# One decoder layer on one core: order of the first loads, merge weights by broadcast loads, 1/rms at the MLP's outputs, weight sums by DMA, and DVE's order at the end

## The chip, the cores and the metric

The kernel runs on one core of a Trainium2 chip. The metric is device time in microseconds (us) of one execution; lower is better. A core has five engines that run side by side, each through its own instructions in order: TensorE (PE: matrix products and transposes), VectorE (DVE), ScalarE (ACT), GpSimd (POOL) and SyncE (SP, which here only issues DMA transfers). They wait for one another through semaphores.

## The reference

One layer of a decoder over 512 tokens of width 1024, all in float32:

```python
h = rmsnorm(x, g_mix)
z = h @ w_in            # 9728 columns: retention q/k/v/gate, attention q/k/v of 3 groups, 2 merge gates
ret_branch = (silu(rg) * rmsnorm(retention(rotate(rq), rotate(rk), rv), ret_gn)) @ w_ret_out
aq, ak = rotate(rmsnorm(aq, q_gain)), rotate(rmsnorm(ak, k_gain))    # per head and group
outs, lses = [dilated_window_attention(aq[g], ak[g], av[g]) for g in 3 groups]
att_branch = sum_g(softmax(lses)[g] * outs[g]) @ w_att_out
x = x + (sig(gl_r + b) * ret_branch + sig(gl_a + b) * att_branch) @ w_o
x = x + square(relu(rmsnorm(x, g_mlp) @ w_up)) @ w_down             # 4096 wide
x = x + sig(rmsnorm(x, g_ple) @ w_ple_gate) * (p @ w_ple_proj)
```

`rmsnorm` divides each token's row by its root mean square and multiplies by a gain for each column.

## The kernel before

**Products.** Each float32 operand is split into two rounded parts, hi (a copy that rounds, on ACT, L228 for weights) and lo (the rest, on DVE, L229), and a product takes three matmuls: hi*hi, lo*hi, hi*lo (L261 to L263). One matmul has a 128 x 128 stationary part and 512 moving columns. Weights come in units of 512 KB (`raw`, 128 x 1024), listed beforehand in a plan; a unit holds 12 such matmuls in the MLP. Six raw buffers and four split buffers (`whi`, `wlo`) run ahead of TensorE: `fetch` issues loads on SP, `ahead` splits two units further than the product at hand has taken.

**Order.** The program is written as it would run on one thread, with a queue of postponed steps (`later(lag, ...)`) that are taken up one at each `tick` between matmuls; `force` brings a step forward. A scheduler then decides each engine's order, except for instructions that `pin` keeps in the order of the program. Each engine runs its list strictly in that order.

**Stages.** `setup` loads the gains as columns (`gcol`), the transposed x (`xr`) beside the first four weight units, and x by tokens (`x`). `load_tables` loads the rotation table (`rotc`), the mask, and, as six broadcast loads, the q and k gains into the tile `mg`, each also with its halves swapped. `first_panel` computes the first 512 columns of z without the norm's factor: 1/rms is a number per token, so it is applied as z leaves PSUM (`zn`, L552). That factor r comes from squares of x on ACT (L484), v on DVE (L487) and a power on POOL (L488). Then for each head the q and k rows are normed (v, r on POOL at L327, `zn` on DVE at L558), rotated (`ro`) with tables C and S (table times gain, L537), transposed by heads (`ph`) and copied (`hT`).

After the first attention group, `embed` loads p transposed (`praw`), splits it (`pT`, L467 and L468) and computes p @ w_ple_proj, which is kept in DRAM (`pp_dram`). Two more groups follow, then retention, during which `merge` weighs the three groups: for each head and group four transposes of a column of weights spread over 128 columns (`pc`, L699) put the weight of each token along the free axis, and DVE multiplies (`mt`, L702). `spread_factors` does the like for r (`r_free`, L497). `mix` computes gates, branch products and their sum; `tail` multiplies by w_o and adds to x.

**MLP.** The norm of x is applied before its transposes: squares on ACT, v and r, y = x * r (L366), four transposes (`pt`, L337), and hi and lo with the gain (L345, L346). The down product is done in four stages of seven products instead of eight (a Strassen-like scheme, `seven_gemm`): its weights are sums and differences of blocks. For a sum, a second raw unit is loaded and DVE adds it (L208); differences are made on DVE too (L205). The products' results are added to x on DVE (L905). As rows of x are complete in the last stage, `ready` starts the last norm and its transposes into h3, and `fin` computes the sigmoid, the product with pp, the sum and the store.

Of the kernel before, what the change touches and what calls it, by code (L numbers as in the profile page):

```python
# [75 lines left out]
class Block:  # L76
# [102 lines left out]
    def fetch(self, n):  # L179
        while len(self.raws) < min(len(self.plan), n):  # L180
# [12 lines left out]
            if add is not None:  # L193
                g0 = self.wraw.tile([P, 1024], F32, tag="raw", name=self.nm("raw2")).rearrange("p (k n) -> p k n", k=k)
                self.nc.sync.dma_start(g0, rows(add[0]))
            self.raws.append((raw, g0))

    def ahead(self, n):
        while len(self.loaded) < min(len(self.plan), self.used + n):
# [4 lines left out]
            if isinstance(src, tuple) and src[0] is None:  # L204
                self.nc.vector.tensor_tensor(raw, raw, self.raws[g0][0], op=ALU.subtract)  # L205
                g0 = None
            elif isinstance(src, tuple):
                self.nc.vector.tensor_tensor(raw, raw, g0, op=ALU.add)  # L208
                g0 = None
# [55 lines left out]
    def rows_gemm(self, act, nk, consume, perm=False, group=2, need=None, halves=False):  # L265
# [3 lines left out]
        for u0 in range(0, nu, group):  # L269
            us = self.units(min(group, nu - u0))  # L270
            for t in range(NT):
                if need is not None:
                    need(t)
# [56 lines left out]
    def split_T(self, src, t, gcol, c, dst):  # L330

        nc = self.nc
        for part in src:
            n = part.shape[1] // P
            ps = self.bank("pt")
# [33 lines left out]

    def new_act(self, nbig, s):  # L370
        return ([self.big(s + "h") for _ in range(nbig)], [self.big(s + "l") for _ in range(nbig)])


    def setup(self):
        nc, a = self.nc, self.a
        self.gcol = self.const.tile([P, 48], F32, name="gcol")
        nc.sync.dma_start(self.gcol, a["vec_cols"])
# [26 lines left out]
    def load_tables(self):  # L404
# [20 lines left out]
    def first_panel(self, consume):  # L425
# [23 lines left out]
        for k in range(KD // 2):  # L449
            for t in range(NT):  # L450
                part(t, k)
        self.token_factors()
        for t in range(NT):
# [3 lines left out]
            self.ahead(1 + t // 2)  # L457
# [3 lines left out]
    def embed(self):  # L461
        nc = self.nc
        pT = self.big("pT")
# [4 lines left out]
        nc.vector.tensor_tensor(R(lo), raw, hi, op=ALU.subtract)  # L468
        self.pp_dram = self.dram.tile([S, D], F32, name="pp_dram", tag="pp_dram")
# [8 lines left out]
    def token_factors(self):  # L478
# [3 lines left out]
        for t in range(NT):  # L482
            j = self.big("j").rearrange("p a b -> p (a b)")[:, :D] if t == 0 else j
            nc.scalar.activation(j, self.x_tiles[t], AF.Square, accum_out=ss[:, t : t + 1])  # L484
# [4 lines left out]
        d = self.dram.tile([S, 1], F32, name="r_dram", tag="r_dram")  # L489
# [4 lines left out]
    def spread_factors(self):  # L494
        ps = self.bank("pc")
# [3 lines left out]
        self.nc.scalar.activation(self.r_free, ps, AF.Copy)  # L499
# [162 lines left out]
    def merge(self, groups, oh, ol):  # L662
# [29 lines left out]
        accs = [None] * H  # L692
        nat = lambda ap: ap.rearrange("p (l r) -> p r l", r=DIL)

        def weigh(h, g):
            self.force(("att", g, NT - 1))
            ps = self.bank("pc")
            for r in range(DIL):
                nc.tensor.transpose(ps[:, r * P : (r + 1) * P],  # L699
                                    cs[g][:, r, h : h + 1].to_broadcast([P, P]), self.ident)  # L700
            t = self.tmp("mt")
            nc.vector.tensor_tensor(t, groups[g][0][:, h], ps, op=ALU.mult)  # L702
# [11 lines left out]
        for h in range(H):  # L714
            for g in range(NG):
                self.later(8, lambda h=h, g=g: weigh(h, g), ("O", h, g))
# [103 lines left out]
    def mix(self, A, O):  # L820
# [61 lines left out]
    def seven_gemm(self, U, xs, ready):  # L882
# [21 lines left out]
        def acc(x, v, op=ALU.add):  # L904
            nc.vector.tensor_tensor(x, x, v, op=op)  # L905
# [5 lines left out]
        for p in range(2):  # L911
# [3 lines left out]
            acc(X(0, 1, p), banks[3, p])  # L915
            acc(X(0, 1, p), banks[5, p], ALU.subtract)
        for u in range(2):
            product(2, 4, u, False, u == 1)
        for p in range(2):
            acc(X(1, 0, p), banks[4, p])  # L920
            acc(X(1, 1, p), banks[4, p], ALU.subtract)
        for u in range(2):
            product(1, 1, u, u == 0, u == 1)
        for p in range(2):
            acc(m4[p], banks[1, p])
            acc(X(0, 0, p), m4[p])
            acc(X(1, 1, p), m4[p])
        for u in range(2):
            product(7, 5, u, False, u == 1)
        for p in range(2):  # L930
            acc(X(0, 0, p), banks[5, p])
            if ready is not None:
                ready(p)
        for u in range(2):
            product(6, 3, u, False, u == 1)
        for p in range(2):
            acc(X(1, 1, p), banks[3, p])
            if ready is not None:
                ready(2 + p)


    def tail(self, mx):
# [59 lines left out]
        for half in range(2):  # L1002
# [70 lines left out]
```

## Time and profile before

| | |
|---|---|
| three runs | 1030.88, 1027.52, 1030.28 us; median 1030.28 |
| profiled execution | 1032.18 us, of which the span (first to last instruction) is 1030.4 |
| TensorE busy | 1010.3 us, 98% of the span |
| DVE, ACT, POOL busy | 654.1, 461.4, 50.3 us |
| mean granted TensorE clock | 0.992 |
| DMA | 130.91 MB, mean 127 GB/s |

How to read the rows. A row of a timeline has the start and duration in us, engine, line, operation, output<-inputs, and in brackets how long the engine had been idle and what ended the wait. A row of groups has line, engine, operation, names, shapes, count, then busy us and mean ns of one, then idle us before them. A window's row has from:to, its length, then for each engine asked for its busy us and count, then the granted clock, the share of time in which the 16 DMA engines were busy, and GB/s. A DMA issue row ends with KB and the median us from issue to landing. In the rows of the chain that ended last, the columns are start, us, and what the time was spent on. Matmuls overlap: a 128x512 matmul lasts 0.39 us in the rows, while the next starts earlier. At half clock it lasts 0.63.

### The profile page before, as it was taken

What the parts mean: (1) busy time and instruction counts of PE and PEld (TensorE: products, weight loads), DVE (VectorE), ACT (ScalarE), POOL (GpSimd) and SP (SyncE); (2) the same over time, 40 slices, a digit from 0 to 9 for tenths busy, and PEclk for the clock granted to TensorE, in tenths of its full rate; (3) what the DMA queues carried; (4) which work ended last, traced back from release to release, by engine and by line L of the source; (5) the groups of instructions that cost most, each with busy time, mean ns of one, the idle gap of its engine ahead of it and who ended that gap; (6) DMA issues with size and microseconds to landing.
All of it is one profiled execution on the core that took longest, in us unless ns stands there. A gap on an engine that the chain in (4) does not pass through costs nothing.

```text
span 1030.4 us, 12593 instructions
## 1 busy us (share of the span) xinstructions
PE 1010.3 (98%) x4778; PEld 847.3 (82%) x4778; DVE 654.1 (63%) x968; ACT 461.4 (45%) x898; POOL 50.3 (5%) x64
## 2 busy tenths in 40 slices
PE   9698999999999999999999999999999999999998
PEld 6587889988988788888888888988888888888877
DVE  4486557666578734555443444679769867867983
ACT  4553545454343332534332323664456355356461
POOL 0110011011000001000110010000000000000000
PEclk9898999999999999999999999999999999999999
DMA  9734322223221241222232431355744753845711
GB/s 319 179 100 138 104 82 82 82 63 122 83 82 41 83 118 46 82 82 82 82 107 98 166 108 54 116 171 174 238 160 136 234 178 117 262 157 189 244 63 56
DMA packets 85869, 130.91 MB, mean 127 GB/s; under 512 B 7472, under 2 KB 39728, under 8 KB 85808
## 3 DMA queue, kind: packets, MB, share of 16 engines
q1 hardware_dynamic: 85808, 130.10, 39.5%
q8 instruction: 37, 0.61, 0.3%
q14 instruction: 24, 0.20, 0.1%
HBM read 125.87 MB, written 4.21 MB: 126 GB/s over the span
## 4 chain that ended last, share of the span: by engine, by line
PE 83%; DVE 9%; DMA 3%; issue 2%; ACT 1%; POOL 1%; SPq 0%; ACTq 0%; DVEq 0%; POOLq 0%
PE pg L261 24%; PE pg L263 24%; PE pg L262 24%; DVE wlo L229 2%; DMA raw<-in_w_in 2%; PE pb L261 2%; PE pb L263 2%; PE pb L262 2%; PE po L640 1%; POOL r L327 1%; PE pt L337 1%; DMA rotc<-in_c_rot 1%; PE ph L523 1%; DVE ro L511 1%; PE sc L617 1%
## 5 line engine op out<-in xcount | busy, mean ns | idle before, releaser
L228 ACT ACTIVATE whi<-raw 128x1024 fp32r<-128x1024 f32 (+1 forms) x198 | 204.3, 1040 | 237.5 <-PE pg L263 100.2
L229 DVE TENSOR_TENSOR wlo<-raw,whi 128x1024 fp32r<-128x1024 f32 (+1 forms) x198 | 239.9, 1221 | 82.0 <-ACT whi L228 80.8
L261 PE MATMUL pg<-whi,hh 128*128 128x512 f32 x480 | 201.1, 420 | 9.1 <-ACT zn L552 8.5
L262 PE MATMUL pg<-wlo,hh 128*128 128x512 f32 x480 | 189.8, 395 | 0.0
L263 PE MATMUL pg<-whi,hl 128*128 128x512 f32 x480 | 189.6, 395 | 0.0
L261 PEld LDWEIGHTS pg<-whi,hh 128*128 128x128 f32 x480 | 99.3, 207 | 24.3 <-ACT zn L552 9.0
L263 PEld LDWEIGHTS pg<-whi,hl 128*128 128x128 f32 x480 | 99.0, 206 | 17.7
L262 PEld LDWEIGHTS pg<-wlo,hh 128*128 128x128 f32 x480 | 99.5, 207 | 14.1 <-DVE wlo L229 0.4
L261 PE MATMUL pg<-h2h,whi 128*128 128x512 f32 (+1 forms) x288 | 105.4, 367 | 0.0
L262 PE MATMUL pg<-h2l,whi 128*128 128x512 f32 (+1 forms) x288 | 105.2, 365 | 0.0
L263 PE MATMUL pg<-h2h,wlo 128*128 128x512 f32 (+1 forms) x288 | 105.2, 365 | 0.0
L327 POOL TENSOR_TENSOR r<-v,mhalf 128x4 f32<-128x4 f32 (+1 forms) x48 | 38.2, 796 | 780.1 <-DVE v L326 780.1
L263 PEld LDWEIGHTS pg<-h2h,wlo 128*128 128x128 f32 x288 | 54.3, 189 | 8.8
L262 PEld LDWEIGHTS pg<-h2l,whi 128*128 128x128 f32 x288 | 54.3, 189 | 8.7
L261 PEld LDWEIGHTS pg<-h2h,whi 128*128 128x128 f32 x288 | 54.2, 189 | 8.6
L261 PE MATMUL pg<-hh,whi 128*128 128x512 f32 x128 | 52.5, 410 | 0.0
L263 PE MATMUL pg<-hh,wlo 128*128 128x512 f32 x128 | 50.0, 390 | 0.0
L262 PE MATMUL pg<-hl,whi 128*128 128x512 f32 x128 | 49.9, 390 | 0.0
L261 PE MATMUL pg<-whi,uh 128*128 128x512 f32 x128 | 49.9, 390 | 0.0
L263 PE MATMUL pg<-whi,ul 128*128 128x512 f32 x128 | 49.9, 390 | 0.0
L262 PE MATMUL pg<-wlo,uh 128*128 128x512 f32 x128 | 49.8, 389 | 0.0
L208 DVE TENSOR_TENSOR raw<-raw,raw 128x1024 f32<-128x1024 f32 x32 | 39.0, 1220 | 11.3 <-DMA raw<-in_w_down 11.2
(179 smaller groups left out, 1669.9 us busy)
## 6 DMA issues: line engine op xcount, KB each, us to landing
raw<-in_w_down SPq DMA_DIRECT2D x80, 512.0 KB, 3.4
raw<-in_w_in SPq DMA_DIRECT2D x72, 512.0 KB, 3.8
raw<-in_w_up SPq DMA_DIRECT2D x32, 512.0 KB, 4.9
x<-in_x SPq DMA_DIRECT2D x8, 512.0 KB, 6.7
raw<-in_w_ret_out SPq DMA_DIRECT2D x8, 512.0 KB, 3.4
raw<-in_w_o SPq DMA_DIRECT2D x8, 512.0 KB, 3.3
raw<-in_w_ple_gate SPq DMA_DIRECT2D x8, 512.0 KB, 4.5
xr<-in_x_cols SPq DMA_DIRECT2D x8, 256.0 KB, 5.4
```

Of the source, the lines that this page charges most:

```text
L208: self.nc.vector.tensor_tensor(raw, raw, g0, op=ALU.add)
L228: self.pin(nc.scalar.activation(R(hi[:, i]), raw[:, i], AF.Copy))
L229: nc.vector.tensor_tensor(R(lo[:, i]), raw[:, i], hi[:, i], op=ALU.subtract)
L261: t.matmul(ps, sh, mh, start=first, stop=False, skip_group_check=more)
L262: t.matmul(ps, sh, ml, start=False, stop=False, skip_group_check=more)
L263: t.matmul(ps, sl, mh, start=False, stop=last, skip_group_check=more)
L327: self.nc.gpsimd.tensor_tensor(r, v, self.mhalf[:, :w], op=ALU.pow)
L337: nc.tensor.transpose(ps[:, k * P : (k + 1) * P], part[:, k * P : (k + 1) * P], self.ident)
L511: nc.vector.tensor_tensor(v4(t2)[:, :, o0 : o0 + 64], v4(zn)[:, :, i0 : i0 + 64], bc(Sn[:, o0 : o0 + 64], 64), op=ALU.mult)
L523: self.nc.tensor.transpose(ps[:, t * P : (t + 1) * P], rots[t][:, h * HD : (h + 1) * HD], self.ident)
L617: nc.tensor.matmul(sc[:, h * P : (h + 1) * P], qT[:, h, rs], kT[:, h, rs], start=True, stop=True)
L640: nc.tensor.matmul(po[:, h * P : (h + 1) * P], v[:, vt, h * HD : (h + 1) * HD], pt, start=b == 0, stop=b == len(blocks) - 1)
```

## The change

Five parts, which share a file but little code.

1. *First loads.* `gcol` is loaded from ACT's queue, and a tiny activation there loads ACT's table early. Weight units 4 and 5 are fetched before the tables (`fetch(6)`). The q and k gains come as one array that the host has arranged, in one broadcast load of 128 x 1536. The four squares are pinned ahead of the splits of units 4 and 5, which are done in halves. The load and split of p are moved from `embed` to `embed_operands`, after the first group's k projection.
2. *Merge weights.* The 48 weights of each token are transposed once, stored to DRAM, and come back as 12 broadcast loads (`cb`), each issued three weighings ahead. `r_free` is a broadcast load of r too.
3. *1/rms at the MLP's outputs.* The MLP's input is x times the gain row (`gr`), not yet divided. Since relu and square pass a positive factor on as its square, the accumulation multiplies each product by f = 1/v or -1/v per token (L948 after); the last norm's factor goes into the sigmoid's scale.
4. *Weight sums by DMA.* The second unit of a sum is added to the first by an accumulating DMA that GpSimd issues into the same buffer; the DVE add and the second buffer are gone.
5. *Order at the end.* From the last stage of `seven_gemm` on, ACT's and DVE's instructions keep the order of the program; halves of x are scaled and transposed as they are complete, some into other banks.

```diff
@@ fetch, ahead
             if add is not None:
-                g0 = self.wraw.tile([P, 1024], F32, tag="raw", name=self.nm("raw2")).rearrange("p (k n) -> p k n", k=k)
-                self.nc.sync.dma_start(g0, rows(add[0]))
+                self.nc.gpsimd.dma_start(raw, rows(add[0]), accum_op=ALU.add)
...
-            elif isinstance(src, tuple):
-                self.nc.vector.tensor_tensor(raw, raw, g0, op=ALU.add)
-                g0 = None
@@ new helpers
+    def gain_T(self, x, t, h, gain, dst, key, lag, bank=None):
+        y = self.tmp("y")
+        self.nc.vector.tensor_tensor(y, x[:, h * 512 : (h + 1) * 512], gain[h], op=ALU.mult)
+        self.later(lag, lambda: self.split_T([y], t, None, 4 * h, dst, bank), (key, t, h))
+    def mean_squares(self, x, v):
+        ss = self.small(2, "ss")
+        for h in range(2):
+            j = self.tmp("j")
+            nc.scalar.activation(j, x[:, h * 512 : (h + 1) * 512], AF.Square, accum_out=ss[:, h : h + 1])
+        s1 = self.small(1, "s1")
+        nc.vector.tensor_tensor(s1, ss[:, 0:1], ss[:, 1:2], op=ALU.add)
+        nc.vector.tensor_scalar(v, s1, 1.0 / D, EPS, op0=ALU.mult, op1=ALU.add)
@@ setup, load_tables
-        nc.sync.dma_start(self.gcol, a["vec_cols"])
+        nc.scalar.dma_start(self.gcol, a["vec_cols"])
...
+        self.fetch(6)
...
+        nc.scalar.activation(warm[:, 500:501], warm[:, 501:502], AF.Copy)
...
-        for n, name in enumerate(("q_gain", "k_gain")):
-            g = a[name][0]
-            nc.sync.dma_start(gv[:, 2 * n], bass.AP(tensor=g.tensor, offset=g.offset, ap=[[0, P], [1, NG * HD]]))
-            for half in range(2):
-                nc.sync.dma_start(
-                    gv[:, 2 * n + 1].rearrange("p (g e) -> p g e", g=NG)[:, :, half * 64 : half * 64 + 64],
-                    bass.AP(tensor=g.tensor, offset=g.offset + 64 * (1 - half), ap=[[0, P], [HD, NG], [1, 64]]))
+        g = a["rot_gains"]
+        nc.sync.dma_start(mg.rearrange("p a b -> p (a b)")[:, 512:],
+                          bass.AP(tensor=g.tensor, offset=g.offset, ap=[[0, P], [1, 4 * NG * HD]]))
@@ first_panel, token_factors
+        self.pinned = True
         self.token_factors()
+        self.ahead(2)
+        self.pinned = False
...
-            self.ahead(1 + t // 2)
...
-            nc.scalar.activation(j, self.x_tiles[t], AF.Square, accum_out=ss[:, t : t + 1])
+            self.pin(nc.scalar.activation(j, self.x_tiles[t], AF.Square, accum_out=ss[:, t : t + 1]))
@@ spread_factors
-        for t in range(NT):
-            self.nc.tensor.transpose(ps[:, t * P : (t + 1) * P], self.r[:, t : t + 1].to_broadcast([P, P]), self.ident)
...
+        self.nc.sync.dma_start(self.r_free, self.r_dram.rearrange("t c -> c t").to_broadcast([P, S]))
@@ attention
+        if g == 0:
+            self.embed_operands()
@@ merge
+        nc.tensor.transpose(ps[: NG * H * NT, :P], wide, self.ident)
...
+        nc.sync.dma_start(cd.rearrange("a (r l) -> (a r) l", r=DIL), turned)
...
+            nc.sync.dma_start(c, cd[g * H + h : g * H + h + 1].to_broadcast([P, S]))
...
-            for r in range(DIL):
-                nc.tensor.transpose(ps[:, r * P : (r + 1) * P],
-                                    cs[g][:, r, h : h + 1].to_broadcast([P, P]), self.ident)
...
-            nc.vector.tensor_tensor(t, groups[g][0][:, h], ps, op=ALU.mult)
+            nc.vector.tensor_tensor(t, groups[g][0][:, h], spread.pop((h, g)), op=ALU.mult)
@@ seven_gemm
-        def acc(x, v, op=ALU.add):
-            nc.vector.tensor_tensor(x, x, v, op=op)
+        def acc(i, j, p, v, sign=0):
+            t, x = 2 * i + p, X(i, j, p)
+            c = sign * NT + t
+            nc.vector.scalar_tensor_tensor(x, v, f[:, c : c + 1], x, op0=ALU.mult, op1=ALU.add)
@@ tail
+        nc.vector.reciprocal(f2[:, :NT], v2)
+        nc.vector.tensor_scalar(f2[:, NT:], f2[:, :NT], -1.0, None, op0=ALU.mult)
...
-                ready = lambda t: self.norm_T(xs[t], t, 24, h3, "h3", 2 if t < 2 else 0)
-            self.seven_gemm(U, xs, ready)
+                def ready(t, j):
+                    late = (t < 2) == (j == 0)
+                    self.gain_T(xs[t], t, j, g3, h3, "h3", 0 if late else 5 - 4 * (t // 2),
+                                None if late else self.gbank)
...
+            if f == NF // 2 - 1:
+                order = self.tc.manual_schedule(engines={nc.scalar.engine, nc.vector.engine})
+                order.__enter__()
+            self.seven_gemm(U, xs, f2, ready)
...
-                nc.scalar.activation(s[:, i], ps[:, i], AF.Sigmoid)
+                nc.scalar.activation(s[:, i], ps[:, i], AF.Sigmoid, scale=r3[:, t : t + 1])
```

How this moves instructions shows at three places. (A number behind a name tells buffers apart; raw_114 and raw_116 after, raw_291 and raw_361 before, are weight units 4 and 5.) First, ACT's order between the first panel's last split and the first eviction zn, before:

```order
L484 ACTIVATE j_242,ss_241<-x_108 128x1024
L228 ACTIVATE whi_293<-raw_291 128x1024
L484 ACTIVATE j_242,ss_241<-x_108 128x1024
L484 ACTIVATE j_242,ss_241<-x_109 128x1024 x2
L228 ACTIVATE whi_363<-raw_361 128x1024
L552 ACTIVATE zn_269<-pg_189,r 128x512
L556 ACTIVATE j_268,ss_267<-zn_269 128x128 x4
```

And after:

```order
L224 ACTIVATE whi_179<-raw_103 128x512
L509 ACTIVATE j_242,ss_241<-x_108 128x1024 x2
L509 ACTIVATE j_242,ss_241<-x_109 128x1024 x2
L224 ACTIVATE whi_255<-raw_114 128x512 x2
L224 ACTIVATE whi_261<-raw_116 128x512 x2
L574 ACTIVATE zn_281<-pg_189,r 128x512
L578 ACTIVATE j_280,ss_279<-zn_281 128x128 x4
```

All four squares (j, ss) now stand ahead of the splits of units 4 and 5; before, three of them stood behind unit 4's.

At the same place, DVE's order from the first panel's last split to the first head norm's v (`v<-ss` after `C` and `S`, the table multiplies), before:

```order
L229 TENSOR_TENSOR wlo_180<-raw_103,whi_179 128x512
L537 TENSOR_TENSOR C_280<-rotc_134,mg_137 128x512
L537 TENSOR_TENSOR S_281<-rotc_134,mg_137 128x512
L229 TENSOR_TENSOR wlo_294<-raw_291,whi_293 128x1024
L537 TENSOR_TENSOR C_400<-rotc_134,mg_137 128x512
L537 TENSOR_TENSOR S_401<-rotc_134,mg_137 128x512
L487 TENSOR_SCALAR v_247<-ss_241 128x4
L229 TENSOR_TENSOR wlo_364<-raw_361,whi_363 128x1024
L326 TENSOR_SCALAR v_275<-ss_267 128x4
```

And after:

```order
L225 TENSOR_TENSOR wlo_180<-raw_103,whi_179 128x512
L559 TENSOR_TENSOR C_292<-rotc_139,mg_142 128x512
L559 TENSOR_TENSOR S_293<-rotc_139,mg_142 128x512
L559 TENSOR_TENSOR C_400<-rotc_139,mg_142 128x512
L559 TENSOR_TENSOR S_401<-rotc_139,mg_142 128x512
L512 TENSOR_SCALAR v_247<-ss_241 128x4
L225 TENSOR_TENSOR wlo_256<-raw_114,whi_255 128x512 x2
L225 TENSOR_TENSOR wlo_262<-raw_116,whi_261 128x512 x2
L322 TENSOR_SCALAR v_287<-ss_279 128x4
```

The factor's v stood behind two table multiplies, a split and two more; now it stands behind all four table multiplies and ahead of the splits.

Second, ACT's order at the k projection of the first group, where p's split now stands; before, from the second tile's eviction on:

```order
L552 ACTIVATE zn_526<-pg_429,r 128x512
L556 ACTIVATE j_525,ss_524<-zn_526 128x128 x4
L144 ACTIVATE hT_399<-ph_588 128x512
L228 ACTIVATE whi_636<-raw_634 128x1024
L552 ACTIVATE zn_570<-pg_442,r 128x512
L556 ACTIVATE j_569,ss_568<-zn_570 128x128 x4
L228 ACTIVATE whi_642<-raw_640 128x1024
L552 ACTIVATE zn_614<-pg_455,r 128x512
```

And after:

```order
L574 ACTIVATE zn_526<-pg_429,r 128x512
L578 ACTIVATE j_525,ss_524<-zn_526 128x128 x4
L488 ACTIVATE pT_633<-praw_634 128x1024
L144 ACTIVATE hT_399<-ph_588 128x512
L224 ACTIVATE whi_641<-raw_639 128x1024
L574 ACTIVATE zn_570<-pg_442,r 128x512
L224 ACTIVATE whi_647<-raw_645 128x1024
L578 ACTIVATE j_569,ss_568<-zn_570 128x128 x4
```

pT stood ten rows on, among the next stage's copies; now it stands ahead of a head's copy hT, of a weight split and of the third tile's zn.

Third, DVE's order in the last down stage, from the second split (wlo) of product 7 to the two splits of product 6, the last. Before:

```order
L229 TENSOR_TENSOR wlo_7805<-raw_7799,whi_7804 128x1024
L208 TENSOR_TENSOR raw_7826<-raw_7826,raw_7828 128x1024
L905 TENSOR_TENSOR m_7730<-m_7730,pb_7785 128x512
L905 TENSOR_TENSOR m_7734<-m_7734,pb_7792 128x512
L905 TENSOR_TENSOR x_4894<-x_4894,m_7730 128x512
L905 TENSOR_TENSOR x_4895<-x_4895,m_7730 128x512
L905 TENSOR_TENSOR x_4894<-x_4894,m_7734 128x512
L905 TENSOR_TENSOR x_4895<-x_4895,m_7734 128x512
L229 TENSOR_TENSOR wlo_7832<-raw_7826,whi_7831 128x1024
L208 TENSOR_TENSOR raw_7847<-raw_7847,raw_7849 128x1024
L905 TENSOR_TENSOR x_4894<-x_4894,pb_7662 128x512
L905 TENSOR_TENSOR x_4894<-x_4894,pb_7669 128x512
```

And after:

```order
L347 TENSOR_TENSOR h3l_7479<-pt_7680,h3h_7477 128x4x128
L225 TENSOR_TENSOR wlo_7691<-raw_7687,whi_7690 128x1024
L347 TENSOR_TENSOR h3l_7478<-pt_7700,h3h_7476 128x4x128
L347 TENSOR_TENSOR h3l_7478<-pt_7713,h3h_7476 128x4x128
L974 TENSOR_TENSOR m_7598<-m_7598,pb_7659 128x512
L948 SCALAR_TENSOR_TENSOR x_4863<-m_7598,f_4882,x_4863 128x512
L948 SCALAR_TENSOR_TENSOR x_4864<-m_7598,f_4882,x_4864 128x512
L974 TENSOR_TENSOR m_7604<-m_7604,pb_7673 128x512
L948 SCALAR_TENSOR_TENSOR x_4863<-m_7604,f_4882,x_4863 128x512
L948 SCALAR_TENSOR_TENSOR x_4864<-m_7604,f_4882,x_4864 128x512
L225 TENSOR_TENSOR wlo_7730<-raw_7726,whi_7729 128x1024
L225 TENSOR_TENSOR wlo_7749<-raw_7745,whi_7748 128x1024
```

The two weight sums (L208) are gone from between; copies of transposes (h3l) have come in ahead of the m adds, each of which waits for a transpose and for ACT's copy. Two m adds and four accumulations still stand ahead of product 6's splits, in another order.

More of the change, by code (lines that the diff above doesn't have):

```diff
@@ L272, in rows_gemm @@
                 if need is not None:
-                    need(t)
+                    need(t, u0)
                 if u0 == 0:
@@ L712, in weigh, with step @@
                 nc.vector.tensor_tensor(R(nat(ol[:, h])), av, nat(oh[:, h]), op=ALU.subtract)
-        for h in range(H):
-            for g in range(NG):
-                self.later(8, lambda h=h, g=g: weigh(h, g), ("O", h, g))
+        items = [(h, g) for h in range(H) for g in range(NG)]
+        for i, (h, g) in enumerate(items):
+            if i == 0:
+                for p in items[:3]:
+                    self.later(4, lambda p=p: load(*p))
+            def step(i=i, h=h, g=g):
+                weigh(h, g)
+                if i + 3 < len(items):
+                    load(*items[i + 3])
+            self.later(8, step, ("O", h, g))
     def ret_proj(self, extra=None):
@@ L914, in seven_gemm @@
             m4.append(t)
-            acc(X(0, 1, p), banks[3, p])
-            acc(X(0, 1, p), banks[5, p], ALU.subtract)
+            acc(0, 1, p, banks[3, p])
+            acc(0, 1, p, banks[5, p], 1)
+            done(0, 1, p)
         for u in range(2):
@@ L919, in seven_gemm @@
         for p in range(2):
-            acc(X(1, 0, p), banks[4, p])
-            acc(X(1, 1, p), banks[4, p], ALU.subtract)
+            acc(1, 0, p, banks[4, p])
+            done(1, 0, p)
+            acc(1, 1, p, banks[4, p], 1)
         for u in range(2):
@@ L930, in seven_gemm @@
         for p in range(2):
-            acc(X(0, 0, p), banks[5, p])
-            if ready is not None:
-                ready(p)
+            acc(0, 0, p, banks[5, p])
+            done(0, 0, p)
         for u in range(2):
@@ L936, in seven_gemm @@
         for p in range(2):
-            acc(X(1, 1, p), banks[3, p])
-            if ready is not None:
-                ready(2 + p)
+            acc(1, 1, p, banks[3, p])
+            done(1, 1, p)
     def tail(self, mx):
@@ L997, in tail, with need @@
                 h3 = self.new_act(2, "h3")
[L998 to L999 removed]
+                halves = [0] * NT
+                def ready(t, j):
+                    late = (t < 2) == (j == 0)
+                    self.gain_T(xs[t], t, j, g3, h3, "h3", 0 if late else 5 - 4 * (t // 2),
+                                None if late else self.gbank)
+                    halves[t] += 1
+                    if halves[t] == 2:
+                        v = self.small(1, "v")
+                        self.mean_squares(xs[t], v)
+                        nc.gpsimd.tensor_tensor(r3[:, t : t + 1], v, self.mhalf[:, :1], op=ALU.pow)
+            if f == NF // 2 - 1:
+                order = self.tc.manual_schedule(engines={nc.scalar.engine, nc.vector.engine})
+                order.__enter__()
+            self.seven_gemm(U, xs, f2, ready)
         out = self.a["out"][0]
         for half in range(2):
+            def need(t, u0):
+                self.force(("h3", t, 0 if u0 < 2 and half == 0 else 1))
             def fin(t, ps, i=slice(0, 512)):
@@ L1009, in fin @@
                 nc.sync.dma_start(out[t * P : (t + 1) * P, c], s[:, i])
-            self.rows_gemm(h3, KD, fin, need=lambda t: self.force(("h3", t, 1)), group=GG[half], halves=half == 1)
+            self.rows_gemm(h3, KD, fin, need=need, group=GG[half], halves=half == 1)
+        order.__exit__(None, None, None)
     def make_plan(self):
@@ L1058 @@
     data.update(shape_constants())
+    qk = []
+    for n in ("q_gain", "k_gain"):
+        g = inputs[n][0].reshape(NG, 2, HD // 2)
+        qk += [g.reshape(-1), g[:, ::-1].reshape(-1)]
+    data["rot_gains"] = np.ascontiguousarray(np.concatenate(qk)[None])
     data["x_cols"] = np.ascontiguousarray(inputs["x"][0].T)
@@ L1061 @@
     data["vec_cols"] = np.ascontiguousarray(np.concatenate(
-        [inputs[n][0] for n in ("g_mix", "ret_gn", "g_mlp", "g_ple", "b_gate")]).reshape(-1, P).T)
+        [inputs[n][0] for n in ("g_mix", "ret_gn", "b_gate")]).reshape(-1, P).T)
     arrays, aps = {}, {}
```

65 lines of the change are left out of this document (47 added, 18 removed).

## The prediction

> **What bounds the kernel now.** I read the page's busy line and slices first, then TensorE's busy time by windows, to see where the one busy engine loses time.
>
> ```profile
> span 1030.4 us, 12593 instructions
> PE 1010.3 (98%) x4778; PEld 847.3 (82%) x4778; DVE 654.1 (63%) x968; ACT 461.4 (45%) x898; POOL 50.3 (5%) x64
> DVE  4486557666578734555443444679769867867983
> PEclk9898999999999999999999999999999999999999
> ...
> 0.00:40.00 40.00, 29.42 (x109) 0.93 0.88 303
> 40.00:140.00 100.00, 96.22 (x457) 0.94 0.38 106
> 140.00:460.00 320.00, 318.76 (x1572) 1.00 0.27 81
> 460.00:960.00 500.00, 500.00 (x2322) 1.00 0.46 149
> 960.00:1030.40 70.40, 65.86 (x324) 1.00 0.32 107
> ```
>
> The window rows give from:to, length, TensorE busy (matmuls), granted clock, DMA share, GB/s. From 460 to 960, TensorE is never idle at full clock: there an edit pays only if it takes matmuls out, however busy DVE is. What can be regained otherwise lies ahead of 140 (14.4 us of idleness and a clock below 1) and after 960, where most of the 4.5 idle us are the last evictions. The timeline and the chain that ended last show the first hole.
>
> ```profile
> 25.14 0.69 DVE L537 TENSOR_TENSOR C<-rotc,mg 128x512 f32<-128x512 f32 x1 [8.02 <-DMA mg<-in_q_gain]
> ...
> 16.95 1.06 ACT L484 ACTIVATE j<-x 128x1024 f32<-128x1024 f32 x1 [0.64 <-DMA x<-in_x]
> ...
> 32.27 1.06 ACT L228 ACTIVATE whi<-raw 128x1024 fp32r<-128x1024 f32 x1 [14.16 <-DMA raw<-in_w_in]
> ...
> 35.58 1.06 ACT L484 ACTIVATE j<-x 128x1024 f32<-128x1024 f32 x1
> ...
> 36.76 0.17 DVE L487 TENSOR_SCALAR v<-ss 128x4 f32<-128x4 f32 x1 [0.97 <-ACT j L484]
> ...
> 38.14 0.69 ACT L552 ACTIVATE zn<-pg,r 128x512 f32<-128x512 f32 x1 [0.47 <-POOL r L488]
> ...
> 38.88 0.80 PE L261 MATMUL pg<-whi,hh 128*128 128x512 f32 x1 [8.54 <-ACT zn L552]
> ```
>
> TensorE waits 8.54 us for the first eviction zn, zn for r, r for four squares, of which three stand behind a split that waits 14.16 us for its weights.
>
> **First loads.** When do r's inputs come now?
>
> ```profile
> 14.33 9.50 DMA rotc<-in_c_rot
> 23.84 8.32 DMA raw<-in_w_in
> ...
> 20.00:24.00 4.00, 4.00 (x19) 3.34 (x18) 0.00 (x0) 0.00 (x0) 0.00 (x0) 1.00 1.10 348
> 24.00:28.00 4.00, 4.00 (x19) 3.30 (x19) 1.39 (x2) 0.00 (x0) 0.00 (x0) 1.00 0.66 150
> ```
>
> The last two numbers of a window row are DMA share and GB/s. The squares stand ahead of the splits in the new order, so ACT is done with them soon after the x tiles. But on DVE the four table multiplies now stand ahead of v, and they need the gain table. Before, rotc had landed by 23.84. Two weight units go ahead of it now: 2 x 512 KB at 348 GB/s = 3.0 us, so 26.8; the mask's 256 KB, 0.75, gives 27.6; the gains' 768 KB take 2.3 at 348 GB/s (landing 29.9) or 5.2 at the 150 that ran while the gains were being spread before (32.8). The queue is fed, and the new rows are 6 KB long rather than up to 1.5, so I take 29.9. From there: four multiplies, 4 x 0.69 = 2.8; v to zn, with POOL's r between, 38.14 - 36.76 = 1.4; zn to the first matmul, 0.7. TensorE restarts at 34.8 rather than 38.88: -4.1. Ends: -6.4 if the gains come along with the mask, -1.2 at 150 GB/s. The new waiter behind this is v, with r, zn, every eviction of the panel and so TensorE queued behind it. The preloaded activation table brings the first matmul about 1 us forward: nothing, since the panel then merely ends earlier and waits longer for zn.
>
> The half clock that follows the restart stays, at no further price: the heads at 58 to 59 waited for DVE anyway, and that chain starts at r and moves with it.
>
> **Embedding.** The hole at 90, and the price of its load:
>
> ```profile
> 91.56 1.06 ACT L467 ACTIVATE pT<-praw 128x1024 fp32r<-128x1024 f32 x1 [4.60 <-DMA praw<-in_p_cols]
> ...
> 92.67 0.80 PE L261 MATMUL pg<-whi,pT 128*128 128x512 f32 x1 [2.78 <-ACT pT L467]
> ...
> 97.51 0.63 PE L262 MATMUL pg<-wlo,pT 128*128 128x512 f32 x1
> 97.94 0.63 PE L263 MATMUL pg<-whi,pT 128*128 128x512 f32 x1
> ...
> 308.62 0.39 PE L261 MATMUL pg<-whi,hh 128*128 128x512 f32 x1
> ...
> 309.76 0.39 PE L263 MATMUL pg<-whi,hl 128*128 128x512 f32 x1
> ...
> praw<-in_p_cols SPq DMA_DIRECT2D x1, 512.0 KB, 6.3
> ```
>
> The wait goes: -2.8. After it the matmuls start 0.43 us apart, still so at 97.94; at full clock, five steps take 309.76 - 308.62, 0.228 each. Over the 6 us from 92.67 on, 0.2 is lost in each 0.43, which is 2.8, and somewhat more until the clock is back: -3.2. Together -6.0.
>
> The Trainium skill ("TensorE: Matmul & The Clock Gate", Part 1) has the clock halve after an idle window of about 3.4 us. By that rule a hole of 2.78 should keep the full clock, and the edit would bring 2.8, the sum ending 3.2 higher. The trace differs: 2.78 us was enough here, so the row stands.
>
> The load is not free at its new place. It stands on SP behind a weight load whose buffer comes free with the second of these two splits, and pT stands on ACT ahead of a head's copy and the next zn:
>
> ```profile
> 58.96 2.27 DVE wlo L229 x2
> ...
> 59.01 0.33 PE L523 MATMUL ph<-ident,ro 128*128 128x128 f32 x1 [0.58 <-DVE ro L513]
> ...
> 63.04 0.60 ACT L144 ACTIVATE hT<-ph 128x512 f32<-128x512 f32 x1 [1.11 <-PE ph L523]
> ```
>
> So it is issued at about 61.2 of before's time and lands 6.3 later at most, while ACT has nothing left ahead of pT from about 62: a stall of up to 5 us, with hT, whi and zn behind it. TensorE has the panel's next tiles to go on with; late are the heads that need hT. I take +0.5, by the 0.58 that such heads cost at 59; ends 0 and 4.6 (ACT's stall at 91 in full).
>
> **Merge weights.** A set of four transposes, then the next matmul, and the groups:
>
> ```profile
> 309.99 0.60 PE L699 MATMUL pc<-ident,c 128*128 128x128 f32 x4
> 310.34 0.48 PE L261 MATMUL pg<-whi,hh 128*128 128x512 f32 x1
> ...
> L699 PE MATMUL pc<-ident,c x48: 270/272/273, 310.0 to 330.5; 128*128 128x128 f32 x48
> ...
> inner<-in_c_dec SPq DMA_DIRECT2D x1, 256.0 KB, 2.8
> ```
>
> From one matmul's start to the next, a set takes 0.35 with up to 0.1 more on the matmul behind it: 0.44. Twelve sets and the like one for r_free: 13 x 0.44 = 5.7, less 0.11 for the one transpose added: -5.6, on a path where TensorE is always busy. The loads that replace them are 12 x 256 KB in a stretch at 81 GB/s; each lands in about 2.8 and is issued three weighings ahead; twelve weighings in 310 to 330 make that 5 us. Covered; without the cover a late one costs up to 2.8 in the branch product that needs O. What is copied on DVE and ACT ahead (four small ops) hides under the gate product.
>
> **1/rms at the outputs, and sums by DMA.** The second norm's chain goes, accumulations carry a factor, and 32 adds leave DVE:
>
> ```profile
> L208 DVE TENSOR_TENSOR raw<-raw,raw 128x1024 f32<-128x1024 f32 x32 | 39.0, 1220 | 11.3 <-DMA raw<-in_w_down 11.2
> ...
> L229 DVE TENSOR_TENSOR wlo<-raw,whi 128x1024 fp32r<-128x1024 f32 (+1 forms) x198 | 239.9, 1221 | 82.0 <-ACT whi L228 80.8
> ...
> L905 DVE TENSOR_TENSOR x<-x,pg 128x512 f32<-128x512 f32 x32 | 20.5, 681 | 0.5 <-PE pg L263 0.5
> ...
> L763 DVE SCALAR_TENSOR_TENSOR G<-pg,r,sg 128x512 f32<-128x512 f32 x8 | 6.0, 750 | 9.0 <-ACT sg L762 9.0
> ...
> raw<-in_w_down SPq DMA_DIRECT2D x80, 512.0 KB, 3.4
> ```
>
> DVE gains 39 us and pays 64 x 0.07 = 4.5; worth 0, since TensorE loses nothing from 460 to 960. The price is an accumulating DMA by GpSimd, which no row shows. A unit holds TensorE for 12 x 0.228 = 2.7 us, and buffers run six units ahead: 16.4. A plain landing of 3.4 and another 3.4 make 6.8. I take 0; the other end is a rival below.
>
> **Order at the end.** In the last stage DVE now follows the program. From the first accumulation to the last two splits of the order rows above, DVE has 12 accumulations x 0.75 = 9.0, ten 512-wide ops (gain multiplies, copies, m adds) x 0.68 = 6.8, six splits and two subtractions x 1.22 = 9.8: 25.6 us, for six units of TensorE, 6 x 2.74 + 4 transpose sets x 0.44 = 18.2. DVE falls 7.4 behind. Before, in the like stretch, 16 accumulations x 0.68 and six splits, three sums and a subtraction x 1.22 made 23.1 for 16.4, so it fell 6.7 behind as well:
>
> ```profile
> 960.00:1000.00 40.00, 39.72 (x187) 1.00 0.43 143
> ```
>
> and lost only 0.3, since splits run ahead and the scheduler chose. With the like cover the wait is 7.4 - 6.4 = 1.0; without any it is 7.4, and the copies of transposes that now stand ahead of splits wait themselves for TensorE and ACT. I take +3.8, a little under the middle, the trace of before being the nearer.
>
> **Sum** against the profiled execution, 1032.18: -4.1 - 6.0 + 0.5 - 5.6 + 3.8 = -11.4, so 1020.8. That execution is 1.9 above the median of the three runs, 1030.28, so I predict 1018.9 for the median.
>
> **Rivals.**
>
> *Accumulating transfers are dear* (slower). Per down stage, 14 units x 2.7 = 38 us, twelve plain loads at 1.5 (512 KB at 348 GB/s) and eight sums at c share the DMA engines: 18 + 8c against 38 + 16 of lookahead, so it decides from c = 4.5, three times a plain load. At four times, c = 6, four stages lose 12 each, +48: 1067. For it: no such transfer is in the trace, and its reading and writing of the buffer could count twice or more. Against: the DMA share is 0.46 there, and twice is covered. 0.13.
>
> *The gain table is the late one*: at 150 GB/s or worse v comes no earlier than now, and the first hole stays. The sum without -4.1: 1023. For it: 25.14's wait of 8.02 on gains. 0.13.
>
> *The tail's waits repeat*: every split of the last stage comes late, the whole 7.4 and half as much again at the transposes, +11 rather than +3.8, with the ACT stall at its 4.6: 1030, no gain to speak of. 0.10.
>
> **Chances.** The forecast has 0.62, the rivals 0.13, 0.13, 0.10; 0.02 is left for the rest. A measurement of this kernel tells 0.3% from no change, that is 3.1 us. Faster: 0.62 + 0.13 + 0.02 of the tail's case = 0.77; same: 0.08, the rest of the tail's case; slower: 0.13 + 0.02 = 0.15. Range: the best ends (-6.4, 0, +1.0) give 1013.3, and the lowest run, 1027.52, was 2.8 below its median, so 1010.5; the upper end takes in the tail's case, 1030.2. Beyond it lie the dear sums.
>
> **What would show it.** Right: TensorE's first wait 4 us or so with DVE's C in front of v as its cause; no half clock at 90; an ACT wait for praw near 60; no pc sets between 300 and 330; 460 to 950 free of idleness; two or three waits of 1 to 2 us for wlo in the last stage. Wrong: waits for raw on in_w_down all over the MLP, a first hole of 8 us, or none at all.

## The result, and the profile after

| | before | after |
|---|---|---|
| median | 1029.52 us (4 runs, 1027.52 to 1030.88) | 1021.76 us (4 runs, 1021.59 to 1022.68) |
| profiled execution, its span | 1032.18, 1030.4 | 1021.85, 1020.1 |

The ratio is 0.9928, 95% interval 0.9909 to 0.9947. Of the page of the kernel after, these lines answer to those shown of before; below them are the two DMA queues and the issues of the down weights, whose sums GpSimd now issues (`q0`, `POOLq`):

```profile
span 1020.1 us, 12454 instructions
PE 1001.6 (98%) x4727; PEld 840.5 (82%) x4727; DVE 620.4 (61%) x895; ACT 452.9 (44%) x853; POOL 86.3 (8%) x92
PEclk9899999999999999999999999999999999999999
q1 hardware_dynamic: 77728, 117.78, 35.9%
q0 software_dynamic: 8704, 16.78, 9.6%
raw<-in_w_down SPq DMA_DIRECT2D x48, 512.0 KB, 3.7
raw<-in_w_down POOLq DMA_DIRECT2D x32, 512.0 KB, 6.9
```

TensorE by windows, the first three cut as before (length, busy us, clock, DMA share, GB/s):

```profile
0.00:40.00 40.00, 33.03 (x125) 0.91 0.83 294
40.00:140.00 100.00, 97.39 (x490) 1.00 0.38 115
140.00:460.00 320.00, 319.13 (x1551) 1.00 0.30 94
460.00:950.00 490.00, 489.68 (x2268) 1.00 0.56 153
950.00:990.00 40.00, 36.37 (x166) 0.96 0.45 130
```

Two stretches before 140 have become better, and a new hole stands at 950 to 990, at a lower clock. Where the time went is seen from the start of one and the same matmul in both traces:

| start of | before | after | shift |
|---|---|---|---|
| first matmul after the first hole | 38.88 | 33.82 | -5.06 |
| first product with pT | 92.67 | 85.15 | -7.52 |
| first product with O (oh) | 453.05 | 436.56 | -16.49 |
| first of the seven products (pg) | 694.12 | 677.89 | -16.23 |
| last of the last stage (uh) | 977.81 | 969.88 | -7.93 |
| last product with h3 | 1025.62 | 1015.50 | -10.12 |

After the embedding the shift is -10.8, so the embedding gave 2.5 ahead of its first matmul and 3.3 behind; the merge gave 5.6 by 453. Then it stays, within 0.3, up to 940, and the last stage gives 8.3 back, of which the last product regains 2.2, since four more sets of transposes for h3 (0.44 each) are done by then than before. The first hole, on DVE, POOL, ACT and TensorE:

```profile
28.98 0.69 DVE L559 TENSOR_TENSOR C<-rotc,mg 128x512 f32<-128x512 f32 x1 [12.91 <-DMA mg<-in_rot_gains]
...
31.40 0.16 DVE L512 TENSOR_SCALAR v<-ss 128x4 f32<-128x4 f32 x1
31.47 2.49 DVE L225 TENSOR_TENSOR wlo<-raw,whi 128x512 fp32r<-128x512 f32 x4
...
31.71 1.33 POOL L513 TENSOR_TENSOR r<-v,mhalf 128x4 f32<-128x4 f32 x1 [30.40 <-DVE v L512]
...
33.08 0.69 ACT L574 ACTIVATE zn<-pg,r 128x512 f32<-128x512 f32 x1 [9.31 <-POOL r L513]
...
33.82 0.79 PE L257 MATMUL pg<-whi,hh 128*128 128x512 f32 x1 [5.50 <-ACT zn L574]
```

It is the new waiter of the prediction: the gains land, four multiplies run, then come v, r and zn. Next p's load, where ACT now waits 6.79 us with TensorE hardly touched, and the embedding, which starts without a wait and at full clock (steps of 0.23):

```profile
63.63 1.06 ACT L488 ACTIVATE pT<-praw 128x1024 fp32r<-128x1024 f32 x1 [6.79 <-DMA praw<-in_p_cols]
...
66.75 0.50 PE L257 MATMUL pg<-whi,hh 128*128 128x512 f32 x1 [0.17 <-ACT zn L574]
...
85.15 0.39 PE L257 MATMUL pg<-whi,pT 128*128 128x512 f32 x1
85.38 0.39 PE L258 MATMUL pg<-wlo,pT 128*128 128x512 f32 x1
```

And the last stage, DVE, then TensorE:

```profile
957.46 0.67 DVE L974 TENSOR_TENSOR m<-m,pb 128x512 f32<-128x512 f32 x1
958.17 1.41 DVE L948 SCALAR_TENSOR_TENSOR x<-m,f,x 128x512 f32<-128x512 f32 x2
959.50 0.68 DVE L974 TENSOR_TENSOR m<-m,pb 128x512 f32<-128x512 f32 x1
960.22 1.41 DVE L948 SCALAR_TENSOR_TENSOR x<-m,f,x 128x512 f32<-128x512 f32 x2
961.55 2.35 DVE L225 TENSOR_TENSOR wlo<-raw,whi 128x1024 fp32r<-128x1024 f32 x2
...
960.00 0.61 PE L257 MATMUL pg<-whi,uh 128*128 128x512 f32 x2
962.82 0.79 PE L258 MATMUL pg<-wlo,uh 128*128 128x512 f32 x1 [2.21 <-DVE wlo L225]
963.41 0.63 PE L259 MATMUL pg<-whi,ul 128*128 128x512 f32 x1
```

TensorE waits for a split that stands behind m adds and accumulations, and the 2.2 us hole brings the half clock (0.63). What the half clock costs is seen in e2 below.

### The profile page after: what moved, and what is told of

The parts are those of the page before. It is cut to its first block, busy times and chain, and to the rows that moved or that the text cites. A ratio compares the mean times of both kernels' runs of the same rounds, so it can differ in the third digit from the quotient of the medians.

```text
span 1020.1 us, 12454 instructions
## 1 busy us (share of the span) xinstructions
PE 1001.6 (98%) x4727; PEld 840.5 (82%) x4727; DVE 620.4 (61%) x895; ACT 452.9 (44%) x853; POOL 86.3 (8%) x92
## 4 chain that ended last, share of the span: by engine, by line
PE 87%; DVE 6%; DMA 3%; ACT 1%; issue 1%; POOL 1%; SPq 0%; ACTq 0%; DVEq 0%; POOLq 0%
PE pg L257 25%; PE pg L258 25%; PE pg L259 25%; PE pb L257 2%; PE pb L259 2%; PE pb L258 2%; DVE wlo L225 1%; PE po L664 1%; DMA mg<-in_rot_gains 1%; PE ph L545 1%; PE pt L333 1%; PE sc L641 1%; DVE x L948 1%; DMA praw<-in_p_cols 1%; PE ry L844 1%
## 5 line engine op out<-in xcount | busy, mean ns | idle before, releaser
L257 PE MATMUL pg<-whi,hh 128*128 128x512 f32 x480 | 199.0, 416 | 5.7 <-ACT zn L574 5.7
L194 POOL DMA_DIRECT2D raw<-in_w_down x32 | 38.8, 1223 | 323.7 <-DMA raw<-in_w_down 256.6
L323 POOL TENSOR_TENSOR r<-v,mhalf 128x4 f32<-128x4 f32 (+1 forms) x40 | 32.9, 822 | 389.5 <-DVE v L322 389.5
```

What stands on the lines that cost most here:

```text
L194: self.nc.gpsimd.dma_start(raw, rows(add[0]), accum_op=ALU.add)
L257: t.matmul(ps, sh, mh, start=first, stop=False, skip_group_check=more)
L323: self.nc.gpsimd.tensor_tensor(r, v, self.mhalf[:, :w], op=ALU.pow)
```

## The experiments

All but e8, which is e2 with one thing more, e10 and the last are the changed kernel with one thing altered. Times are medians, ratios stand against the kernel before on the same chip.

| | us | ratio, interval |
|---|---|---|
| e1_free_order | 1019.21 | 0.9894, 0.9879 to 0.9909 |
| e2_r_first | 1019.98 | 0.9903, 0.9887 to 0.9920 |
| e3_transposed_weights | 1028.45 | 0.9981, 0.9971 to 0.9990 |
| e4_embed_late | 1026.83 | 0.9973, 0.9961 to 0.9985 |
| e5_sums_on_dve | 1033.57 | 1.0031, 1.0017 to 1.0044 |
| e6_zeros_added | 1077.21 | one run |
| e7_halves_later | 1022.09 | 0.9920, 0.9903 to 0.9936 |
| e8_v_ahead | 1016.19 | 0.9857, 0.9838 to 0.9875 |
| e9_low_parts_first | 1022.02 | 0.9914, 0.9897 to 0.9930 |
| e10_repeat (the change itself) | 1022.33 | 0.9920, 0.9905 to 0.9935 |
| e11_differences_early | 1017.41 | 0.9872, 0.9857 to 0.9886 |
| e12_together | 1010.86 | 0.9808, 0.9794 to 0.9823 |

**The merge and the embedding, undone one by one.** e3:

```diff
-        nc.tensor.transpose(ps[: NG * H * NT, :P], wide, self.ident)
...
-            nc.vector.tensor_tensor(t, groups[g][0][:, h], spread.pop((h, g)), op=ALU.mult)
+            for r in range(DIL):
+                nc.tensor.transpose(ps[:, r * P : (r + 1) * P],
+                                    cs[g][:, r, h : h + 1].to_broadcast([P, P]), self.ident)
+            nc.vector.tensor_tensor(t, groups[g][0][:, h], ps, op=ALU.mult)
```

> The changed kernel with the 48 transposes for the merge weights, and those for r, as before the change. Theory A: TensorE is busy all the time there, so 52 transposes at 0.11 us less the one that goes come back in full: 5.6 us more, 1027 to 1028 us. Rival B: the broadcast loads, or the queue they share with the weights, cost part of the gain; then less than 4 us comes back, under 1025.8 us.

The first product of the seven starts 5.85 us later than in the changed kernel; 0.26 of that stands ahead of the merge, so 5.6 come back there: theory A, though the median lies 0.45 above its range. The loads cost TensorE nothing.

e4:

```diff
-        if g == 0:
-            self.embed_operands()
...
     def embed(self):
+        self.embed_operands()
```

> The changed kernel with p's load and split back at the start of the embedding. Theory A: the wait of 2.8 us and the half clock behind it, 3.2 us, come back, less the 0.5 us that the early load costs: 5 to 6 us more, 1026.8 to 1028 us. Rival B: only the wait comes back, the clock stays full: 2 to 3 us more, 1024 to 1025 us.

```profile
87.83 0.74 PE L257 MATMUL pg<-whi,pT 128*128 128x512 f32 x1 [2.85 <-ACT pT L488]
88.38 0.63 PE L258 MATMUL pg<-wlo,pT 128*128 128x512 f32 x1
```

The hole and the half clock are both back, 4.7 us from there on: theory A, a little under the 5 to 6 that it named. The half clock lasted 3.4 us here (87.92 to 91.34) and 6.8 in the kernel before (92.21 to 99.04). The Trainium skill ("TensorE: Matmul & The Clock Gate", Part 1) asks for about 3.4 us of idleness; here again the trace differs, and 2.85 are enough.

**The first hole.** e2 pins v and r ahead of the table multiplies:

```diff
         self.token_factors()
         self.ahead(2)
+        self.first_tabs = [self.tables(0, n, True) for n in range(2)]
         self.pinned = False
...
+        if g == 0 and not pin:
+            return self.first_tabs[n]
```

> The changed kernel with v, and so r, ahead of the table multiplies on DVE. Both theories: TensorE's wait for the first zn, 5.5 us, shrinks below 1, as r is there at about 23 us. Theory A, the hole is what counts: all that follows moves with it, 1016 to 1017 us. Rival B, DVE's chain of head norms counts: it cannot start before the tables at 31.4 and takes its 20 us as before, so TensorE only runs ahead to the first heads and waits there, 4 to 6 us at about 45, and 1 to 4 us are gained in all: 1018 to 1020.8 us.

The hole of 5.50 is gone, and another has opened at the first heads:

```profile
50.20 0.33 PE L546 MATMUL ph<-ident,ro 128*128 128x128 f32 x1 [4.03 <-DVE ro L536]
```

Everything behind comes 2.66 us earlier up to the last stage, and the end 2.73: rival B. Behind the wait for r stood DVE's chain of head norms.

This trace also prices the half clock of the last stage. ACT, DVE and TensorE have the same order there as in the changed kernel, and the same hole, but the clock stays full:

```profile
960.36 0.50 PE L258 MATMUL pg<-wlo,uh 128*128 128x512 f32 x1 [2.19 <-DVE wlo L225]
```

TensorE leaves the stage 1.4 us earlier for it, then waits 0.82 us for h3, and the end gains 0.3 at most: DVE sets the time there, and its instructions start 2.5 to 2.7 us earlier throughout.

e8 shortens that chain: of each tile of the first panel, v stands ahead of the tile before's multiply, so that POOL's power runs beside DVE's rotation (`finish` is a tile's multiply by r and its rotation):

```diff
+            held.append(finish)
+            if t:
+                held[t - 1]()
```

> The kernel of e2 (r ahead of the tables, 1020.0 us) with v of the next tile ahead of the multiply of each tile in the first panel, so that POOL's power runs beside DVE's rotation. Theory: the chain on DVE sets the first heads; three of its four waits of 1.12 us for POOL go, so heads and all behind them come 3 us earlier: 1016 to 1017.5 us. Rival: ACT's norms (about 2 us a tile) or TensorE itself then set the time, and less than 1 us comes of it: 1019 to 1020.5 us.

```profile
47.35 0.33 PE L548 MATMUL ph<-ident,ro 128*128 128x128 f32 x1 [2.61 <-DVE ro L538]
```

The heads come 2.9 us earlier still. Three of DVE's four waits for POOL (1.12 us each) are gone, 3.4 in all, and the gains landed 0.3 later in this run. The chain is what counts at the start: e2, which leaves it as it was, gains little, and e8, which shortens it, gains what was taken out.

In the profiles of e5, e6 and e7, the first zn came 1.8 us later than in the others, with the same program up to there. The cause is r, on POOL. In e7, DVE and POOL:

```profile
31.80 2.50 DVE L226 TENSOR_TENSOR wlo<-raw,whi 128x512 fp32r<-128x512 f32 x4
...
32.05 3.14 POOL L514 TENSOR_TENSOR r<-v,mhalf 128x4 f32<-128x4 f32 x1 [30.74 <-DVE v L513]
```

r ends 0.89 us after DVE's four subtractions, a little under the 1.03 that the power takes alone. e9 puts these ahead of the tables:

```diff
-        self.token_factors()
+        ss = self.token_squares()
         self.ahead(2)
+        self.first_tabs = [self.tables(0, n, True) for n in range(2)]
+        self.token_factors(ss)
```

> The changed kernel with DVE's four subtractions for units 4 and 5 ahead of the table multiplies and v, so that DVE has nothing to do while POOL computes r. In the profiles so far that r took 1.03 us where DVE was idle beside it, 1.33 or 3.13 where these subtractions (2.5 us in a row) ran beside it. Theory A: POOL's read waits for DVE's subtractions; r takes 1.03 here whatever the repeat shows, TensorE's first wait is 5.2 to 5.5 us, and the time is 1020 to 1021.8 us. Rival B: r's length is the chip's or the run's, and r is as long here as in the repeat.

> The changed kernel itself once more, on the chip of e9. By theory A of e9 the first r takes 1.33 or 3.13 us by who comes first, and the time is 1021.5 or about 1023.5 us; by B it is as long as in e9.

```profile
31.91 1.03 POOL L519 TENSOR_TENSOR r<-v,mhalf 128x4 f32<-128x4 f32 x1 [30.60 <-DVE v L518]
```

r took 1.03 in e9 and 1.33 in e10. That speaks for A in r's length. The rest of A's forecast was missed: in e9 TensorE waited 6.26 us, not 5.2 to 5.5, and the times of e9 and e10 do not differ. The 3.13 did not come on this chip. All three profiles with it are from one chip, that of e5 to e8, so what decides between 1.33 and 3.13, the order of arrival or the chip, stays open.

**The last stage.** e1 takes the fixed order away:

```diff
-            if f == NF // 2 - 1:
-                order = self.tc.manual_schedule(engines={nc.scalar.engine, nc.vector.engine})
-                order.__enter__()
```

> The changed kernel without the fixed order at the end: ACT and DVE are ordered by the scheduler there, all else is kept. The changed kernel takes 1021.8 us, and its TensorE loses about 8 us between 940 and 990. Theory A, the order: the splits come late because the program's order puts them behind accumulations; with the scheduler free the loss falls to 1 to 3 us, 1016 to 1018 us. Rival B, the work: the gain multiplies and the copies of transposes, which are new inside the last stage, overfill DVE in whatever order; the loss stays above 5 us, 1020 to 1022.5 us.

```profile
954.01 0.66 PE L333 MATMUL pt<-ident,y 128*128 128x128 f32 x4 [2.23 <-DVE h3l L347]
...
962.25 0.50 PE L258 MATMUL pg<-wlo,uh 128*128 128x512 f32 x1 [1.64 <-DVE wlo L225]
```

From the first of the seven products on, this gains 2.8 us by the end, and 3.9 us of waits remain in these two rows: neither theory alone. e7 takes work out instead and keeps the order:

```diff
+                    if t < 2 and j == 1:
+                        self.later(LAG, lambda: self.gain_T(xs[t], t, j, g3, h3, "h3", 3))
...
```

(`LAG` is 16.)

> The changed kernel with two of the four early halves (rows 0 and 1, columns 512 to 1023) put off by 16 ticks, into the last product, where their columns are needed only half way; the order at the end stays fixed. Theory B, the work: two gain multiplies and two copies, 2.7 us of DVE, and two sets of transposes leave the last stage; TensorE's loss there falls from 8 to about 5, 1018 to 1019.5 us. Rival A, the order alone: no more than 1 us is gained, 1020.5 to 1022 us.

By the time alone, rival A. But this execution had the long r and came into the last stage 2.53 us late; it left the seven products 1.68 us early, and of these 4.2 us it gave 2.2 back in the last product, where the two sets of transposes (0.44 each) now stand. So the work counts, and part of it is only moved. e11 moves the differences:

```diff
-            if isinstance(src, tuple) and src[0] is None:
-                self.nc.vector.tensor_tensor(raw, raw, self.raws[g0][0], op=ALU.subtract)
+            if isinstance(src, tuple):
                 g0 = None
             self.loaded.append(self.split_unit(raw, g0))
+            after = self.plan[i + 2][0] if i + 2 < len(self.plan) else None
+            if isinstance(after, tuple) and after[0] is None:
+                self.nc.vector.tensor_tensor(raw, raw, self.raws[after[2]][0], op=ALU.subtract)
```

> The changed kernel with each weight difference on DVE directly behind the split of its first block, rather than when its own split is due; the order at the end stays fixed. Theory: in program order a difference, ACT's rounding and DVE's remainder follow one another, and DVE idles 1.2 us twice in the last stage and does the differences late; without that TensorE's loss there falls from 8 to 4 us: 1017 to 1019 us. Rival: DVE has more than enough to wait for elsewhere, less than 1 us is gained: 1021 to 1022.5 us.

In the changed kernel, DVE idles before each remainder of a difference, with ACT's rounding between:

```profile
941.49 1.22 DVE L204 TENSOR_TENSOR raw<-raw,raw 128x1024 f32<-128x1024 f32 x1
943.91 1.23 DVE L225 TENSOR_TENSOR wlo<-raw,whi 128x1024 fp32r<-128x1024 f32 x1 [1.21 <-ACT whi L224]
945.05 1.22 DVE L204 TENSOR_TENSOR raw<-raw,raw 128x1024 f32<-128x1024 f32 x1
947.48 1.22 DVE L225 TENSOR_TENSOR wlo<-raw,whi 128x1024 fp32r<-128x1024 f32 x1 [1.21 <-ACT whi L224]
```

The theory holds: with the differences made earlier, both idle stretches are gone from DVE, TensorE leaves the seven products 5.6 us earlier, and the end comes 4.3 earlier.

**The sums.** e5 puts them back on DVE:

```diff
-                self.nc.gpsimd.dma_start(raw, rows(add[0]), accum_op=ALU.add)
+                self.nc.sync.dma_start(g0, rows(add[0]))
...
+                self.nc.vector.tensor_tensor(raw, raw, g0, op=ALU.add)
```

> The changed kernel with the weight sums as before: a second plain load into its own buffer, and the add on DVE. Theory A: DVE's time is worth nothing where TensorE never waits, so up to 940 nothing changes; in the last stage, where TensorE waits for DVE, three or four adds of 1.22 us come on top: 3 to 5 us more, 1024.5 to 1027 us. Rival B: the sums by DMA are worth nothing anywhere, 1021 to 1023 us. Rival C: the sums by DMA slow the loads; without them the kernel gets faster, below 1021 us.

TensorE in three stretches, in e5 and then in the changed kernel:

```profile
460.00:940.00 480.00, 480.00 (x2229) 1.00 0.47 150
940.00:990.00 50.00, 42.03 (x165) 0.86 0.46 154
```

```profile
460.00:940.00 480.00, 480.00 (x2228) 1.00 0.56 152
940.00:990.00 50.00, 46.05 (x206) 0.97 0.52 143
```

Theory A in kind: nothing up to 940, all of it in the last stage. Its size was missed: 9.4 us there by the end, not 3 to 5 (of the rest of the 11.8, the long r is 1.7). The adds were counted without what stands behind each of them. DVE in e5:

```profile
954.62 1.22 DVE L208 TENSOR_TENSOR raw<-raw,raw 128x1024 f32<-128x1024 f32 x1
957.03 1.23 DVE L229 TENSOR_TENSOR wlo<-raw,whi 128x1024 fp32r<-128x1024 f32 x1 [1.20 <-ACT whi L228]
```

As with the differences, DVE idles through ACT's rounding. Four adds of the last stage cost 2.4 us each so, 9.6 in all. So with the order at the end fixed as it is, and without sums by DMA, the other four parts together bring nothing: 1.0031, of which the long r is 0.0017.

e6 doubles their price (the second sum adds zeros):

```diff
                 self.nc.gpsimd.dma_start(raw, rows(add[0]), accum_op=ALU.add)
+                self.nc.gpsimd.dma_start(raw, rows(self.a["zeros"][0:256, 0:512]), accum_op=ALU.add)
```

> The changed kernel with a second accumulating transfer behind each sum, which adds zeros: a sum's price is doubled, the result unchanged. By the shares of the two queues a plain 512 KB takes 1.6 us of the 16 DMA engines' time and an accumulating one 3.1. Theory A, the bound of the prediction: a down stage has 12 x 1.6 + 8 x 6.2 = 69 us of transfers against 38 of work and 16 of lookahead, 14 lost in each of four stages and TensorE waits on sums: 1050 to 1085 us. Rival B: the DMA engines have room for it, and only the longer landing counts, 3.7 + 2 x 8 = 20 us against 16.4 of lookahead: a few us for the first sums of a stage, 1025 to 1040 us. Rival C: all of it hides, below 1025 us.

```profile
ACT whi L225 <- DMA raw<-in_zeros: 88.7, 14, 9.8
...
680.00:730.00 50.00, 39.33 (x158) 0.90 0.83 186
```

The size is theory A's, +55. Its mechanism is not shown: the DMA engines were busy 0.83 of this window, not all of it, and GpSimd, in order, cannot issue the next sum while it waits for the landing of the one that it adds zeros to. That wait is the experiment's own, and it came to 138.3 us. So the edit shows that a second transfer behind each sum no longer hides, and leaves open whether the DMA engines or GpSimd's order set the price.

**Together.** e12 has e7, e8 and e11 in one:

> The changed kernel with r ahead of the tables and v of the next tile ahead (e8), two halves later (e7) and differences early (e11). If the causes are separate their gains add: 5.6 at the start, about 6 of the 8 us in the last stage, 1009 to 1012 us. Rival: what is won in the last stage is given back as waits for h3 at the start of the last product, 1013 to 1016 us.

```profile
span 1008.4 us, 12457 instructions
...
0.00:40.00 40.00, 38.54 (x160) 1.00 0.91 303
...
940.00:980.00 40.00, 39.45 (x188) 1.00 0.46 133
```

1010.86 us: 5.8 at the start, and 5.8 of the 6.1 in the last stage. The causes are separate, and this version beats both kernels.

## Why the prediction was right, point by point

The forecast was 1018.9 in a range of 1010.5 to 1030.2, and 1021.76 lies in it. That range reaches from 20 us of gain to none, so the terms tell more. The sum had -11.4 against the profiled execution; it became -10.3. By medians the gain is only 7.8: the profiled execution of before stood 2.7 above its median, that of the changed kernel 0.1, so the 1.9 that the prediction took off to come to a median was not there to be taken. That the sum came out so near is in part luck, since the first loads gave 1.0 more and the order at the end cost 2.3 more than forecast.

- *First loads*, -4.1: -5.06. The gains landed at 28.9, not 29.9: the queue ran at 372 to 382 GB/s from 22 to 30, not at 348. The waiter and its chain are as told. What was not told is the reason why more can't be had here by r alone: e2.
- *Embedding*, -6.0 and +0.5: -5.8 with the early load's price in it, 0.3. e4 gives 4.7. ACT's wait was 6.79, longer than the 5 that was named, as the load took 7.0 and not 6.3, and still hidden.
- *Merge*, -5.6: -5.6, and 5.6 by e3.
- *Sums by DMA*, 0: right in the stretch that the row was taken from, 460 to 960, and no more. A sum lands 6.9 us after its issue, not 3.4, which still fits; it takes (9.6% of 1020)/32 = 3.1 us of the DMA engines where a plain unit takes 1.6, so c = 3.1 against the bound of 4.5, and the slower rival failed by that. But the DVE time that the sums free is worth 9.4 us where TensorE waits for DVE, in the last stage. The prediction counted the adds out of the stage and never asked what the stage would be with them in.
- *Order at the end*, +3.8, within 1.0 to 7.4: +6.1. This is the term that was mis-sized. DVE's backlog was counted as busy time, without the 2.4 us in which it idles between a difference and its remainder (e11). The half clock behind the hole of 2.21, left out too, is worth 0.3 at most (e2). The named cause, the order alone, is less than half of the 6.1 (e1 gains 2.8); the rest is work and its place (e7, e11).

## What to carry to other kernels

When a wait is removed, follow the chain that stands behind it to the next engine, and make that chain's price the bound of the gain: here, in e2, r came 10 us earlier and all behind the heads only 2.7. Work taken from an engine off the critical path is worth nothing in most stages and much in the one stage where that engine is late, so read its price there, by putting the work back. In a fixed order, look for neighbours that wait for each other by way of another engine, count the wait with the work (2.4 us for an add of 1.22 here), and move the first of them up.

## What the hardware showed

- An accumulating DMA of 512 KB, issued by GpSimd: 1.20 us of GpSimd, 5.5 to 11.2 us to landing (median 6.9), 1.9 times the plain transfer's time on the DMA engines.
- In the windows in which the broadcast load of the gains came in, in rows of 6 KB and with other loads beside it, the DMA engines moved 372 and 382 GB/s; in the window of the six loads before, in pieces of 1.5 KB and less, 150.
- A small POOL operation beside DVE subtractions took 1.33 or 3.13 us rather than 1.03; 3.13 came three times in nine profiles, each time on the same chip.
- The clock halved after holes of 2.2 us (the changed kernel, at 962.8) and 2.85 us (e4), but not after one of 2.23 us (e1, at 954.0, where the clock of 950 to 990 was 1.00). What differs is where the hole falls. In all these traces, start and end of the program aside, the half clock lasts 3.41, 6.83 or 10.24 us, one to three steps of 3.41. In every step at full clock with 1.85 us of idleness or more (e8 has the least), the clock was half in the next; with 1.78 or less (e1), it stayed full. The changed kernel's hole lies in one step, e1's across two. Two steps of the changed kernel, then two of e1 (a step's idleness is its length less TensorE's busy time):

```profile
959.38:962.79 3.41, 1.23 (x6) 1.00 0.25 94
962.79:966.20 3.41, 3.38 (x8) 0.50 0.63 193
950.15:953.56 3.41, 1.63 (x9) 1.00 1.09 231
953.56:956.98 3.42, 2.97 (x15) 1.00 0.73 246
```
